# Attention stage: the last matmul of a dense bank and the bank's end are taken from the filler in one go

## The chip, the cores and the metric

One core of a Trainium2 chip runs the whole kernel. The metric is device time in microseconds (us), from one launch. The engines are PE (matmuls; its weight loads are shown apart, as PEld), DVE, ACT, POOL and SP; SP only issues transfers here.

## The reference

One encoder layer over 2048 tokens of width 1024, in float32. A vector `c` gives shift, scale and gate for two sub-layers. The first sub-layer projects the normalised input to queries, keys and values of 16 heads, 8 of them stick-breaking attention and 8 a chunked softmax attention over a band, and projects the joined outputs back; the second is a squared-ReLU MLP.

```python
h = rmsnorm(x, g_norm1) * (1.0 + sc1) + sh1
q_sb, k_sb, v_sb, q_ca, k_ca, v_ca = split(h @ w_in)
o_sb = stick_breaking_attention(q_sb, k_sb, v_sb)
o_ca = chunked_relpos_attention(rmsnorm(q_ca, g_q), rmsnorm(k_ca, g_k), v_ca, rel_bias)
x = x + gt1 * (concat(o_sb, o_ca) @ w_o)
h = rmsnorm(x, g_norm2) * (1.0 + sc2) + sh2
x = x + gt2 * (square(relu(h @ w1)) @ w2)
```

## The kernel before

The tokens are reversed and cut into four blocks of 512 (numbered g, or tb, 0 to 3). Each float32 operand is split into a high and a low part, and each product is three matmuls (high by high, high by low, low by high). The kernel runs in three stages.

In the **first** stage most of the projection is computed for blocks 3 and 2, and part of it for 1 and 0. In the **last** stage the output projection of block 0 runs, and then the MLP, in a form with fewer multiplications (seven products for eight).

Between them lies the **attention**. It is a list of 112 units (one head with one block of queries, and for stick-breaking also one block of keys), each of four steps, and a loop over 448 steps and 8 more that drain the pipeline. In each step PE gets, in this order: the transposes of weights from a unit some steps back (`transposes`, tile `wt`), the products with the values (`values`, tile `acc`), the scores of the next step (`scores`, tiles `z`, `ct`, `cz`), and then what `fill` puts there. DVE, ACT and POOL do the scan or the softmax and evict the transposes. The instructions of PE, ACT, DVE and POOL stay in the order of the program. The transfers issued in the attention by plain `nc.sync` have no such rule; those behind it (`osp`) have.

`fill` takes **dense** matmuls out of generators, the fillers: the projections that the first stage left (`fill_qkv`, twice: 288 matmuls for block 1 and 384 for block 0), and then the output projections of blocks 3, 2 and 1 (`outproj`, 192 matmuls each, eight rows of 24). A dense bank is one PSUM tile of 24 matmuls of 512 columns. The generator yields 1.0 behind each matmul; behind the 24th it yields a function, the bank's end, which evicts the bank. Two PSUM tiles serve as dense banks in turn. Some other yields are words: "wait" rests a step ahead of a new filler.

How many matmuls a step takes is counted in `credit`. Each step adds its share (`shares`, from a model of how much DVE and PE work the step has by itself), in proportion to the dense `work` that is still to be done; of older credit at most `CAP` = 5 is kept. `fill` then pulls from the generator while the credit is at least 1. When it pulls a bank's end, the function is put into `soon` (the jobs of the next step) and `rest = 1` stops the pulling for this step; the next `fill` lowers `rest` to 0 and goes on.

So there are two cases at the end of a bank. If credit is left after the 24th matmul, the bank's end is pulled in the same step. If less than 1 is left, the loop ends behind the 24th matmul; the next step's first pull then gets the bank's end, and that step rests and takes no dense matmul. Its share stays in the credit, up to the cap.

A bank's end of `fill_qkv` is `keep`: through `soon` and `heavy` an ACT copy of the bank is emitted, a step later the DVE subtraction and the store. That of `outproj` is `finish_row`: the DVE instruction `residual` on the row's tile, a store of the row, and for blocks 2 and 3 the sums of squares.

The total of dense matmuls that the attention is to take, `work`, is 14 x 48 + 480 = 1152, or 48 banks. That ends with row 3 of block 1's output projection. Rows 4 to 7 run behind the attention: `row()` pulls from the same generator until it gets one bank's end, and takes one matmul more. Between these calls stand the loads of the next stage's operands: `steps[0].fetch` (tiles `opm`), and the blocks of `right_blocks` (`some(k, n)`: n = 0 loads four tiles `ty`, for k = 0, or `cy`; n = 1 normalises them; n = 2 and 3 make the operands `h` of the MLP):

```python
steps[0].fetch(0, KT // 2)
row()
some(0, 0)
row()
steps[0].fetch(KT // 2, KT - 2)
some(0, 1)
row()
...
```

Of the kernel before, what the change touches and what calls it, by code (L numbers as in the profile page):

```python
# [24 lines left out]
KT = D // P  # L25
# [54 lines left out]
def encoder_kernel(ctx, tc, xs, c, g1, g2, w_in, w_first, w_rest, gqk, bias, w_o, w1, w2, w_ada, b_ada, out):  # L80
# [121 lines left out]
    def norm_apply(which, x, k, dst, pl, tg):  # L202

        j = 3 * which * KT + k
        a, b = aff[:, which, k : k + 1], mod[:, j : j + 1]
        hi, lo = dst[k][:, 0, :], dst[k][:, 1, :]
        act.activation(x, x, AF.Identity, scale=a, bias=b)
        act.copy(hi, x)
        return lambda: dve.tensor_tensor(lo, x, hi.bitcast(F32), op=ALU.subtract) and None
# [23 lines left out]
    def load_residual(g, n, pl):  # L233
        xr = temp(f"xr{g}_{n}") if drain else pl.tile([P, TB], F32, tag="xr", name=f"xr{g}_{n}")
        sp.dma_start(xr, xs[g, :, n])
        return xr
# [7 lines left out]
    if True:  # L244
# [371 lines left out]
        for k in range(KT):  # L616
# [5 lines left out]
            rest = norm_apply(0, xts[3][k], k, hts[3], np_, "a3") if k else None  # L622
            for j in ((KT + k + 1, k + 1) if k else (1,)) if k + 1 < KT else ():
                ada_column(j, adas[j])
                if rest:
                    rest = rest()
# [42 lines left out]
        credit = 0.0  # L669
# [67 lines left out]
    if True:  # L737
# [60 lines left out]
        def keep(u, o):  # L798

            os = fp.tile([P, 2, TB], F32R, tag="st", name=f"os{u.nm}")  # L800
            split(os[:, 0, :], os[:, 1, :], o, pool)
            q = pool if u.ca and u.g == 0 else sp
            q.dma_start(scr_m[u.g, u.ca * 4 + u.h // 2], os.bitcast(F32))
            if u.ca and u.h == NH - 1 and u.g > 0:
                filler.append(Filler(outproj, u.g))
# [240 lines left out]
        def fill_qkv(self, tb, ht, pieces):  # L1046
# [47 lines left out]
            for at, (n, j) in enumerate(banks):  # L1094
                piece, w = pieces[n], parts[n]
                last = at + 1 == len(banks) or not banks[at + 1][1]
                nm = f"f{tb}_{piece}_{j}"
                ps = dense.tile([P, TB], F32, tag="ps", name=f"p{nm}")
                cl = slice(j * P, (j + 1) * P)
                for k in range(KT):  # L1100
                    for m, job in plan.pop((at, k), ()):
                        parts[m].update(job())
                    if at + 1 == len(banks) and k in (0, 4):
                        yield "ahead"
                    for i, (a, b) in enumerate(((0, 0), (0, 1), (1, 0))):
                        flags = {"start": k == 0 and i == 0, "stop": k == KT - 1 and i == 2}
                        if piece in wide:
                            pe.matmul(ps, ht[k][:, b, cl], w[k][:, a, :], **flags)
                        else:
                            pe.matmul(ps, w[k][:, a, cl], ht[k][:, b, :], **flags)  # L1110
                        yield 1.0

                def keep(piece=piece, j=j, ps=ps, nm=nm, last=last):
                    if piece not in wide:
                        st = fp.tile([P, 2, TB], F32R, tag="st", name=f"st{nm}")
                        act.copy(st[:, 0, :], ps)
                        halves = [(st[:, 0, :], st[:, 1, :], ps)]
                    else:
                        if j % 2 == 0:
                            svs[:] = [  # L1120
                                fp.tile([P, NH // 2, 2, 2, HD], F32R, tag="st", name=f"sv{nm}_{hf}") for hf in range(2)
                            ]
                        halves = [
                            (
                                sv[:, :, j % 2, 0, :], sv[:, :, j % 2, 1, :],
                                ps[:, hf * CW : (hf + 1) * CW].rearrange("p (h d) -> p h d", d=HD),
                            )
                            for hf, sv in enumerate(svs)
                        ]
                        for hi, lo, half in halves:  # L1130
                            act.copy(hi, half)
                    parts = list(svs)

                    def rest():
                        for hi, lo, half in halves:
                            dve.tensor_tensor(lo, half, hi.bitcast(F32), op=ALU.subtract)
                        if piece not in wide:
                            at = (0, tb, piece % 2 * 2 + j)
                            to = scr_k[at].rearrange("l d t -> d l t") if piece // 2 else scr_q[at]
                            sp.dma_start(to, st.bitcast(F32))  # L1140
                        elif j % 2:
                            for hf, sv in enumerate(parts):
                                sp.dma_start(
                                    scr_v[piece // 6, tb, hf][:, :, j - 1 : j + 1, :].rearrange("h p t e -> p h (t e)"),
                                    sv.rearrange("p h t l d -> p h (t l d)").bitcast(F32),
                                )
                        if last:
                            have.add((piece, tb))

                    soon.append(rest)  # L1150

                keep.bank = True
                yield keep

        def outproj(self, g):
            def load(n):
                w = ring.tile([P, 2, KT, P], F32R, tag="r8", name=f"ow{g}_{n}")
                sp.dma_start(w.bitcast(F32), scr_wo[n,])
                return w

            self.loaders = [lambda n=n: load(n) for n in range(2)]
            yield lambda k: scr_m[g, k]
            mx = self.moving()
            ws = self.first()
            rx = load_residual(g, 0, xrp)
            yield "wait"
            for n in range(KT):
                w, xr = ws.pop(0), rx
                if g == 1:
                    resident[n] = w  # L1170
                if n + 2 < KT:
                    ws.append(load(n + 2))
                if n + 1 < KT:
                    rx = load_residual(g, n + 1, xrp)
                ps = dense.tile([P, TB], F32, tag="ps", name=f"po{g}_{n}")
                for k in range(KT):
                    if n + 1 == KT and k in (0, 4):
                        yield "ahead"
                    for i, (l, m) in enumerate(((0, 0), (0, 1), (1, 0))):
                        pe.matmul(  # L1180
                            ps, w[:, l, k, :], mx[k][:, m, :], start=k == 0 and i == 0, stop=k == KT - 1 and i == 2
                        )
                        yield 1.0
                yield lambda n=n, ps=ps, xr=xr: finish_row(g, n, ps, xr)

        def finish_row(g, n, ps, xr):
# [59 lines left out]
        def step_shares(units, work):  # L1246
# [32 lines left out]
            return [max(0.15, scale * v - t) for v, t in zip(vector, own)]  # L1279

        filler = [Filler(fill_qkv, 1, hts[1], (2, 3, 10, 0, 1)), Filler(fill_qkv, 0, None, (2, 3, 4, 10, 0, 1))]
        work = 14 * 48.0 + 5 * KT * KT * 3 / 2
        shares = step_shares(units, work)
        weight = sum(shares)
        credit = 0.0
        rest = 0
        late, soon, first, heavy, urgent = [], [], [], [], []

        def fill(part, more=0):

            nonlocal credit, rest, work, weight
            credit = min(credit, CAP) + part * (work - credit) / (weight * 0.95) + more
            weight -= part
            rest = max(0, rest - 1)
            while credit >= 1 and filler and not rest:
                got = next(filler[0].gen, None)
                if got is None:
                    filler.pop(0)
                elif got == "ahead":
                    for f in filler[1:2]:  # L1300
                        f.ahead()
                elif callable(got):
                    soon.append(got)
                    rest = 1
                elif got in RESTS:
                    rest = RESTS[got]
                else:
                    credit -= got
                    work -= got

        def force(f):

# [45 lines left out]
        for i in range(len(steps) + LAG):  # L1358
# [36 lines left out]
            if i + 1 < len(steps):  # L1395
                u, st = steps[i + 1]
                u.scores(st)
            fill(shares[i], turns.get(i, 0))
            later.tick()
        for u, j in late:  # L1400
# [26 lines left out]
    if True:  # L1427
# [610 lines left out]
        for mb in (1, 0):  # L2038
# [22 lines left out]
            if mb:  # L2061
# [11 lines left out]
                rest = len(steps)  # L2073
# [144 lines left out]
```

## Time and profile before

| | us |
|---|---|
| time, median of 3 runs (lowest, highest) | 2507.99 (2507.59, 2508.48) |
| profiled execution: its own time | 2507.11 |
| profiled execution: its span | 2505.4 |
| attention in the profile, first scores to last values | 410 to 1267 |

Of the span, PE is busy 2495.8 us, PEld 2095.3, DVE 2028.2, ACT 1527.0 and POOL 789.6. The granted clock is 0.999. The attention holds 672 dense matmuls into `pf` (the projections) and 480 into `po` (the output projections); 96 more into `po` follow it, between 1266.95 and 1288.8 us.

In the rows of the profile, nearly all instructions carry one line, that of a helper, so groups are told apart by their tiles. A PE row's duration is longer than the distance to the next start, because matmuls are pipelined: 512 columns are shown with some 390 ns, and the next matmul starts 227 ns later.

### The profile page before, as it was taken

To read this page: it belongs to the slowest core of one execution; us is meant where nothing else is said; L and a number is where in the kernel's file an instruction comes from. 1 tells how busy PE (TensorE), PEld (TensorE's weight loads), DVE (VectorE), ACT (ScalarE), POOL (GpSimd) and SP (SyncE) were. 2 spreads that over 40 slices of the span, in tenths; PEclk is the share of its full clock that TensorE was granted. 3 is DMA by queue.
4 is the path that set the end of the run, shared out by engine and by line. 5 is a ranking of instruction groups with operands and counts; after the bars stand their busy time and mean duration, and the time that the engine had idled before them with its cause. 6 is when DMAs were issued, how large, how long until landed. Compare 5 with 4: busy or idle time off the path is not lost.

```text
span 2505.4 us, 39519 instructions
## 1 busy us (share of the span) xinstructions
PE 2495.8 (100%) x12364; PEld 2095.3 (84%) x12364; DVE 2028.2 (81%) x3572; ACT 1527.0 (61%) x2928; POOL 789.6 (32%) x1175
## 2 busy tenths in 40 slices
PE   9999999999999999999999999999999999999999
PEld 8888888888888898888888888888888888888887
DVE  7656776897789888999877777779877859799998
ACT  6334434778876687666755555567555546577765
POOL 4330144777776677776720000000000000010100
PEclk9999999999999999999999999999999999999999
DMA  9879978789888788866787878996998996888982
GB/s 370 317 300 362 354 279 289 230 265 314 259 269 260 234 256 263 263 207 211 221 334 242 302 284 301 351 345 192 325 328 269 316 362 262 320 249 281 302 281 84
DMA packets 296114, 704.71 MB, mean 281 GB/s; under 512 B 32096, under 2 KB 88672, under 8 KB 284256
## 3 DMA queue, kind: packets, MB, share of 16 engines
q1 hardware_dynamic: 287552, 684.22, 79.2%
q0 software_dynamic: 6912, 13.63, 2.9%
q10 hardware_dynamic: 1440, 4.33, 0.4%
q8 instruction: 98, 1.61, 0.3%
q14 instruction: 112, 0.92, 0.1%
HBM read 473.99 MB, written 228.07 MB: 280 GB/s over the span
## 4 chain that ended last, share of the span: by engine, by line
PE 97%; DVE 2%; ACT 1%; issue 0%; DMA 0%; POOL 0%; SPq 0%; DVEq 0%; ACTq 0%; POOLq 0%
PE ps L42 29%; PE ps_s L42 17%; PE pt L42 11%; PE acc L42 8%; PE wt L42 7%; PE pf L42 6%; PE po L42 5%; PE z L42 5%; PE pq L42 3%; PE cz L42 2%; PE pso L42 2%; PE ct L42 1%; PE px L42 1%; DVE p L42 0%; DVE opr L42 0%
## 5 line engine op out<-in xcount | busy, mean ns | idle before, releaser
L42 ACT CAST wth<-wt 128x512 fp32r<-128x512 f32 (+3 forms) x544 | 257.8, 484 | 173.3 <-PE wt L42 160.9
L42 PE MATMUL ps<-h,opw 128*128 128x512 f32 x1512 | 358.6, 389 | 0.0
L42 POOL TENSOR_TENSOR b<-p 128x512 f32<-128x512 f32 (+1 forms) x320 | 292.6, 914 | 153.2 <-DVE p L42 97.2
L42 DVE TENSOR_TENSOR wtl<-wt,wth 128x512 fp32r<-128x512 f32 (+3 forms) x544 | 291.3, 547 | 60.5 <-ACT wth L42 56.1
L42 PEld LDWEIGHTS ps<-h,opw 128*128 128x128 f32 x1512 | 283.7, 188 | 58.8
L42 PE MATMUL pt<-w,ht 128*128 128x512 f32 x1248 | 288.1, 391 | 0.0
L42 PE MATMUL ps_s<-h,opw 128*128 128x512 f32 x1152 | 277.0, 389 | 0.0
L42 PEld LDWEIGHTS pt<-w,ht 128*128 128x128 f32 x1248 | 233.0, 188 | 47.5
L42 DVE TENSOR_TENSOR_SCAN p<-z,p,zero 128x512 f32<-128x512 f32 x192 | 245.2, 1278 | 18.6 <-ACT z L42 14.7
L42 PEld LDWEIGHTS ps_s<-h,opw 128*128 128x128 f32 x1152 | 216.0, 188 | 45.0
L42 ACT CAST opr<-r 128x512 fp32r<-128x512 f32 x280 | 174.3, 623 | 118.1 <-PE ps L42 65.6
L42 PE MATMUL acc<-wth,v 128*128 128x512 f32 (+3 forms) x544 | 221.2, 410 | 0.0
L42 PE MATMUL ps<-opr,ol 128*128 128x512 f32 x960 | 220.3, 389 | 0.0
L42 PEld LDWEIGHTS ps<-opr,ol 128*128 128x128 f32 x960 | 180.1, 188 | 37.8 <-DVE opr L42 0.4
L42 ACT ACTIVATE z<-z 128x512 f32<-128x512 f32 (+1 forms) x320 | 166.6, 521 | 52.7 <-PE z L42 48.9
L42 DVE TENSOR_TENSOR opr<-r,opr 128x512 fp32r<-128x512 f32 x280 | 185.7, 684 | 13.7 <-ACT opr L42 12.5
L42 PE MATMUL acc<-wtl,v 128*128 128x512 f32 (+3 forms) x544 | 185.5, 347 | 0.0
L42 PE MATMUL z<-k,q 128*128 128x512 f32 (+3 forms) x640 | 182.7, 367 | 0.6 <-DVE p L42 0.6
L42 POOL DMA_DIRECT2D scr_x<-txu x12 | 10.4, 869 | 543.5 <-ACT txu L42 541.6
L42 PE MATMUL ps<-oph,opv 128*128 128x512 f32 x768 | 174.9, 389 | 0.2 <-DVE txo L42 0.2
L42 PE MATMUL wt<-ident,b 128*128 128x128 f32 x1088 | 170.7, 272 | 0.4 <-DVE p L42 0.4
L42 PEld LDWEIGHTS ps<-oph,opv 128*128 128x128 f32 x768 | 144.1, 188 | 30.5 <-DVE txo L42 0.6
(238 smaller groups left out, 5064.6 us busy)
## 6 DMA issues: line engine op xcount, KB each, us to landing
r<-scr_hid SPq DMA_DIRECT2D x80, 512.0 KB, 7.5
q<-scr_q SPq DMA_DIRECT2D x128, 256.0 KB, 5.1
w<-in_w_dram SPq DMA_DIRECT2D x64, 512.0 KB, 5.7
k<-scr_k SPq DMA_DIRECT2D x240, 128.0 KB, 4.6
v<-scr_v SPq DMA_DIRECT2D x120, 256.0 KB, 4.3
wa<-in_w_ada_dram SPq DMA_DIRECT2D x48, 512.0 KB, 6.2
ow<-scr_wo SPq DMA_DIRECT2D x24, 1024.0 KB, 6.5
l<-scr_t SPq DMA_DIRECT2D x20, 1024.0 KB, 8.3
```

The source lines that it names most:

```text
L42: return lambda *x, **y: self.tc.keep_in_program_order(f(*x, **y))
```

## The change

The generators mark the last matmul of a bank, and `fill` pulls the bank's end together with it, whatever credit is left. The rest is then set in the step of the last matmul, and not in the step behind it. The matmul counts as one, as before.

```diff
@@ fill_qkv
-                        yield 1.0
+                        yield "last" if flags["stop"] else 1.0
@@ outproj
-                        yield 1.0
+                        yield "last" if k == KT - 1 and i == 2 else 1.0
@@ fill
                 elif got in RESTS:
                     rest = RESTS[got]
                 else:
-                    credit -= got
-                    work -= got
+                    credit -= 1
+                    work -= 1
+                    if got == "last":
+                        soon.append(next(filler[0].gen))
+                        rest = 1
```

`force`, which `row()` uses, is left as it was: it asks only whether what it got can be called.

## The prediction

> **What bounds the kernel now.** I read the page first, then the stages, then what PE waits for in the attention.
>
> ```profile
> span 2505.4 us, 39519 instructions
> PE 2495.8 (100%) x12364; PEld 2095.3 (84%) x12364; DVE 2028.2 (81%) x3572; ACT 1527.0 (61%) x2928; POOL 789.6 (32%) x1175
> ...
> PE 97%; DVE 2%; ACT 1%; issue 0%; DMA 0%; POOL 0%; SPq 0%; DVEq 0%; ACTq 0%; POOLq 0%
> ```
>
> PE is busy for all but 9.6 us of the span, and the chain that ended last is PE for 97%. The change adds and removes no matmul. So it can only win what PE loses by waiting, and can only cost what it makes PE wait. The next view gives the busy time of each engine (columns: PE, PEld, DVE, ACT, POOL, each with its instructions; then clock, share and rate of the DMAs) in the 856 us of attention and in 856 us of the last stage, which has nothing but dense matmuls on PE.
>
> ```profile
> 410.00:1266.00 856.00, 854.23 (x5005) 732.89 (x5004) 748.40 (x1511) 621.59 (x1338) 616.16 (x888) 1.00 0.80 250
> 1345.00:2201.00 856.00, 855.79 (x3789) 708.34 (x3788) 664.95 (x1082) 495.41 (x872) 21.07 (x30) 1.00 0.87 301
> ```
>
> In the attention PE is idle for 856.00 - 854.23 = 1.77 us. DVE is the next engine, with 748.40 / 856 = 87%. The view of PE's waits, for 405 to 1267 us, says who ends them (total, times, longest):
>
> ```profile
> PE z L42 <- DVE p L42: 0.6, 2, 0.3
> PE wt L42 <- DVE p L42: 0.4, 1, 0.4
> PE cz L42 <- DVE cols L42: 0.4, 1, 0.4
> ```
>
> DVE ends all that are listed; no transfer and no eviction of a dense bank is among them.
>
> **The change part by part.** First, how often it does anything. A step without dense matmuls, right behind a bank's 24th, is the case that it alters. Going through PE's timeline and counting `pf` and `po`, I find 19 such steps in the 456, at 48 bank ends. (Four more empty steps follow the end of a filler: there the rest is the new filler's own "wait", which stays. In other steps the share is below one matmul, which stays too.) The first of the 19 starts at 432.57, the last at 1205.21. PE's timeline (start, duration, instruction, count) at the first:
>
> ```profile
> 432.34 0.39 PE L42 MATMUL pf<-ht,fw 128*128 128x512 f32 x1
> 432.57 0.60 PE L42 MATMUL wt<-ident,b 128*128 128x128 f32 x4
> 432.93 0.48 PE L42 MATMUL acc<-wth,v 128*128 128x512 f32 x1
> 433.24 0.39 PE L42 MATMUL acc<-wtl,v 128*128 128x512 f32 x1
> 433.47 0.63 PE L42 MATMUL z<-k,q 128*128 128x512 f32 x2
> 433.94 0.49 PE L42 MATMUL wt<-ident,b 128*128 128x128 f32 x3
> ...
> 435.20 1.53 PE L42 MATMUL pf<-ht,fw 128*128 128x512 f32 x6
> 436.56 0.27 PE L42 MATMUL wt<-ident,b 128*128 128x128 f32 x1
> ```
>
> The reader is to see two things. The empty step takes 433.94 - 432.57 = 1.37 us, with no gap: each row begins where a row of its kind lets the next begin. And the step behind it takes six dense matmuls, twice the usual three: the share was carried, not lost. With the change these would be three and three. One dense matmul takes (436.56 - 435.20) / 6 = 0.227 us, so 3 x 0.227 = 0.68 us of PE work move one step ahead, and by that alone the time doesn't alter. At the last of the 19 it does:
>
> ```profile
> 1204.52 0.86 PE L42 MATMUL po<-fx,ow 128*128 128x512 f32 x3
> 1205.21 0.60 PE L42 MATMUL wt<-ident,e 128*128 128x128 f32 x4
> ...
> 1206.83 0.49 PE L42 MATMUL wt<-ident,e 128*128 128x128 f32 x3
> ...
> 1207.57 0.69 PE L42 MATMUL ct<-k,q 128*128 128x256 f32 x4
> 1208.62 0.62 PE L42 MATMUL cz<-k,q 128*128 128x384 f32 x2 [0.36 <-DVE cols L42]
> 1209.08 1.09 PE L42 MATMUL po<-fx,ow 128*128 128x512 f32 x4
> ...
> 1236.35 0.69 PE L42 MATMUL ct<-k,q 128*128 128x256 f32 x4
> 1236.88 0.51 PE L42 MATMUL cz<-k,q 128*128 128x384 f32 x2
> ```
>
> Without its dense matmuls PE runs ahead, and `cz` waits for a score bank that DVE has not read. From `ct` to `cz` it takes 1208.62 - 1207.57 = 1.05 us, against 1236.88 - 1236.35 = 0.53 us where nothing is late: 0.52 us lost, of which the profile calls 0.36 idle. Three matmuls more in the step at 1205.21 would bring PE there 0.68 us later, which covers the 0.52.
>
> **The gain** lies between nothing (all 19 like the first) and 19 x 0.52 = 9.9 us (all like the last). I take 1.2 us, two thirds of the 1.77 us that the profile calls idle in the whole stage, since that row is the nearest: some of the 1.77 stands at steps that the change doesn't touch.
>
> The other terms. A bank's end is emitted one step earlier in 19 cases: an ACT copy, a DVE subtraction and a store for a projection, one DVE instruction and a store for a row. No such instruction is added. They lie beside PE's matmuls, as the waits above show, and cost nothing; if that cover is gone, one of them delays a score bank by its own length, 0.75 us for a row's (1272.68 below). The loads of dense weights hang on positions within a bank and come at most a step earlier. I cost them at nothing; if a weight comes late, PE waits.
>
> The third term lies **at the end of the attention**. The 48th bank is row 3 of the last output projection. Its last matmul is taken in the last steps, its end before the change only by the first `row()`: DVE's timeline has `residual` of row 3 at once, of row 4 at 1272.68, of row 5 at 1278.84. After the change row 3's end is taken in the attention, so that each call of `row()` reaches one row further, and everything between the calls is queued a row later.
>
> ```profile
> 1272.68 0.75 DVE L42 SCALAR_TENSOR_TENSOR xr<-po,mod,xr 128x512 f32<-128x512 f32 x1 [5.31 <-PE po L42]
> 1276.41 2.51 DVE L42 TENSOR_TENSOR ty<-ty,r 128x512 f32<-128x512 f32 x4 [2.98 <-DMA ty<-scr_x]
> 1278.84 0.74 DVE L42 SCALAR_TENSOR_TENSOR txr<-po,mod,txr 128x512 f32<-128x512 f32 x1
> 1280.62 1.29 DVE L42 TENSOR_TENSOR h<-ty,h 128x512 fp32r<-128x512 f32 x2 [1.04 <-ACT h L42]
> ...
> 1289.45 2.63 DVE L42 TENSOR_TENSOR cy<-cy,r 128x512 f32<-128x512 f32 x4 [1.29 <-DMA cy<-scr_x]
> ...
> 1327.08 0.75 DVE L42 SCALAR_TENSOR_TENSOR cxr<-pso,mod,cxr 128x512 f32<-128x512 f32 x1 [1.89 <-PE pso L42]
> 1327.74 0.68 DVE L42 TENSOR_TENSOR opr<-w,opr 128x512 fp32r<-128x512 f32 x1
> ```
>
> ```profile
> 1259.07 1.80 SPq L42 DMA_DIRECT2D opm<-scr_m  x4
> ...
> 1267.03 1.98 SPq L42 DMA_DIRECT2D ty<-scr_x  x4
> 1272.67 0.32 SPq L42 DMA_DIRECT2D ow<-scr_wo  x1
> 1273.03 0.54 SPq L42 DMA_DIRECT2D txr<-in_xs_dram  x1
> ```
>
> ```profile
> 1266.95 22.00 PE L42 MATMUL po<-fx,ow 128*128 128x512 f32 x96
> 1288.80 16.48 PE L42 MATMUL pso<-opm,ow 128*128 128x512 f32 x72
> ...
> 1332.32 5.60 PE L42 MATMUL ps<-h,opr 128*128 128x512 f32 x24
> ```
>
> On SP the four `ty` loads pass behind the next row's `ow`, which waits for its buffer until 1272.67, and behind `txr`: they go out at about 1273.6 instead of 1267.03, 6.5 us later. From issue to DVE's first product took 1276.41 - 1267.03 = 9.4 us, so that product starts at about 1283. The last part of `h` for k = 0 is then queued behind row 7's `residual`, which waits for PE until 1288.80. I count k = 0 done near 1294.5, and the `cy` products of k = 1 there instead of at 1289.45: some 5 us late. k = 2 and 3 follow without a gap that could take this up, until the wait of 1.89 us at 1327.08. The first operand's DVE part, at 1327.74, would come some 3.2 us later and end at 1327.74 + 3.2 + 0.68 = 1331.6. PE needs it at 1332.32. So this costs nothing, by a margin of 0.7 us: if it is wrong by more, PE waits for the excess. What hides it is the 43.5 us of `pso` in front.
>
> **Sum**: 2507.11 (the profiled execution; 1.7 of it lies around the span) - 1.2 + 0 + 0 = 2505.9 us. The median of the runs stands 0.88 us above the profiled one, so the forecast for the median is 2507.99 - 1.2 = 2506.8 us.
>
> **The rivals.** *The empty steps are lost time.* If each had cost PE the 0.68 us of its share, the change would win 19 x 0.68 = 13 us: 2495. For it speaks only that the busy share can hide idling behind modelled ends. Against it are the burst of six, and start distances of 0.227 us in it. The Trainium skill (Perfetto Trace Analysis, Identifying the Most-Contended Engine) says that the matmul's busy share is a bad measure of how near PE is to its limit, and points to the weight loads' share instead. By that, 1 - 732.89 / 856 = 14% of the attention, over 100 us, could be free, and a large gain with it. The trace doesn't agree that this is headroom: the last stage, a plain stream of matmuls, shows 708.34 / 856 = 83%.
>
> *The late operand chain*, the one that ends slower. It decides from a lateness of 5 + 0.7, rounded up to 5.8 us, at k = 1. If the `ty` loads take their 9.4 us twice, because `opm` and `ow` are in flight as well, k = 0 ends 9.4 us later than I count, 5 + 9.4 - 5.8 = 8.6 us beyond the cover, and PE waits that long at 1332: 2506.8 + 8.6 = 2515.4. For it speaks that the queue is full there. Against it: four of the eight `opm` loads are out before 1267 already, since SP has nothing in front of them.
>
> *A late weight or a worse order elsewhere.* The attention's transfers are placed anew when matmuls move. One wait for a weight would be new; by the longest landing for `ty` above, under 9.4 us, in the middle 4: 2510.8. Against it: not one transfer is among PE's waits.
>
> *The change does nothing that counts.* DVE sets the pace at those waits, so what PE does not lose in the empty step it loses in the next: 2508.0. For it speaks DVE's 87%; against it, that nothing waits in the step behind 1209.08.
>
> **How the numbers follow.** Forecast (0 to 2.5 us gained): 0.68. Does nothing: 0.13. Late chain: 0.07. Late weight: 0.08. Lost time: 0.04. A measurement of this kernel can tell about 0.2%, 5.0 us, from no change. Faster than 2503.0: lost time, and a little of the forecast's upper bound of 9.9 us: 0.05. Slower than 2513.0: most of the late chain and the long end of the late weight: 0.07. The rest, 0.88, is within. The range reaches beyond the forecast into the 9.9 us, to 2503.5, and to the late weight's 2510.8, rounded to 2511.0; the late chain and the lost time lie outside.
>
> **What would show it.** Right: none of the 19 steps empty, no burst of six behind them, and some of the short waits such as that at 1208.62 gone; PE's idle time in the attention under 1.77 us; `ty` issued near 1273.6 and its product near 1283, and no wait of PE at the first `ps<-h,opr`. Wrong: an attention shorter by more than 2 us (hidden idling), PE idle before `ps<-h,opr` (late chain), or a transfer among PE's waits.

## The result and the profile after

The kernel became slower: 2513.51 us (median of 11 runs, 2512.78 to 2516.22) against 2507.99 us (11 runs). The ratio is 1.0024, 95% interval 1.0016 to 1.0032. The forecast was 2506.8 us, with a range from 2503.5 to 2511.0.

The page of the kernel after, to be laid beside that of before; the profiled execution took 2514.01 us:

```profile
span 2512.3 us, 39515 instructions
PE 2498.0 (99%) x12364; PEld 2096.3 (83%) x12364; DVE 2027.3 (81%) x3572; ACT 1527.8 (61%) x2928; POOL 788.6 (31%) x1175
...
PE 91%; DVE 4%; DMA 2%; ACT 2%; issue 1%; SPq 0%; POOL 0%; DVEq 0%; ACTq 0%; POOLq 0%
```

PE has the same 12364 matmuls. A part of the chain that ended last is now a transfer. The view of PE's waits, from the attention to 1290 us, names it:

```profile
PE po L42 <- DMA ow<-scr_wo: 4.2, 1, 4.2
PE z L42 <- DVE p L42: 0.6, 2, 0.3
PE wt L42 <- DVE p L42: 0.4, 1, 0.4
PE ct L42 <- DVE cols L42: 0.2, 1, 0.2
```

**The attention does what was forecast.** PE's timeline at the first and at the last of the 19 places:

```profile
432.08 0.40 PE L42 MATMUL pf<-ht,fw 128*128 128x512 f32 x1
432.32 0.60 PE L42 MATMUL wt<-ident,b 128*128 128x128 f32 x4
...
433.69 0.85 PE L42 MATMUL pf<-ht,fw 128*128 128x512 f32 x3
...
435.63 0.86 PE L42 MATMUL pf<-ht,fw 128*128 128x512 f32 x3
...
1205.68 0.86 PE L42 MATMUL po<-fx,ow 128*128 128x512 f32 x3
...
1207.11 0.69 PE L42 MATMUL ct<-k,q 128*128 128x256 f32 x4
1207.72 0.62 PE L42 MATMUL cz<-k,q 128*128 128x384 f32 x2
```

Three and three stand where none and six stood. From `ct` to `cz` it takes 0.61 us where it took 1.05. None of the 19 steps is empty. The four at the ends of fillers are, and so is one at 762.49, which takes no dense matmul in the kernel before either (762.65).

**The loss lies right behind it.** SP's timeline (start, duration, instruction, count), and PE's, at the end of the attention:

```profile
1266.49 0.32 SPq L231 DMA_DIRECT2D scr_x<-xr  x1
1266.86 1.87 SPq L42 DMA_DIRECT2D opm<-scr_m  x4
1268.83 0.52 SPq L42 DMA_DIRECT2D ow<-scr_wo  x1
1269.45 0.69 SPq L42 DMA_DIRECT2D txr<-in_xs_dram  x1
1271.77 0.32 SPq L42 DMA_DIRECT2D ow<-scr_wo  x1
1272.14 1.26 SPq L42 DMA_DIRECT2D txr<-in_xs_dram  x1
1273.46 4.51 SPq L42 DMA_DIRECT2D ty<-scr_x  x4
```

```profile
1266.06 11.12 PE L42 MATMUL po<-fx,ow 128*128 128x512 f32 x48
1281.35 12.72 PE L42 MATMUL po<-fx,ow 128*128 128x512 f32 x48 [4.18 <-DMA ow<-scr_wo]
1293.92 6.28 PE L42 MATMUL pso<-opm,ow 128*128 128x512 f32 x27
```

The four `opm` loads, out at 1259.07 before, now go out at 1266.86. In front of them stands `scr_x<-xr`, the store of row 3, which waits for DVE's `residual` of row 3:

```profile
1265.72 0.74 DVE L42 SCALAR_TENSOR_TENSOR xr<-po,mod,xr 128x512 f32<-128x512 f32 x1
```

That row ends at 1266.46, and the store goes out at 1266.49. Row 6's weights, `ow`, follow them at 1268.83, and PE has them 12.5 us later, at 1281.35. PE is done with row 5 at about 1277 and waits 4.18 us. Then it loses more: the 48 matmuls from 1281.35 take 1293.92 - 1281.35 = 12.57 us, where 48 x 0.227 = 10.9 us would do. The view of stretches shows why (length; PE, PEld, DVE, ACT and POOL busy, each with its instructions; then the granted clock as a share of full speed, the DMA share and the rate in GB/s):

```profile
1258.00:1267.00 9.00, 9.00 (x62) 8.12 (x61) 5.87 (x14) 7.70 (x19) 3.68 (x4) 1.00 0.34 117
1267.00:1275.00 8.00, 8.00 (x37) 6.59 (x36) 0.75 (x1) 1.13 (x2) 5.72 (x6) 1.00 0.95 323
1275.00:1290.00 15.00, 10.82 (x41) 8.52 (x40) 4.29 (x7) 3.62 (x6) 0.00 (x0) 0.89 1.03 417
1282.31:1285.72 3.41, 3.41 (x9) 2.64 (x8) 0.57 (x2) 0.00 (x0) 0.00 (x0) 0.50 1.02 393
```

The wait ends at 1281.35; from 1282.31 on the granted clock is 0.50 for 3.41 us. And the DMA engines stand two thirds idle between 1258 and 1267 us. The same view of the kernel before, in the first three stretches, for PE alone (length; PE busy; clock, DMA share, rate):

```profile
1258.00:1267.00 9.00, 9.00 (x65) 1.00 0.74 244
1267.00:1275.00 8.00, 8.00 (x38) 1.00 1.02 410
1275.00:1290.00 15.00, 15.00 (x68) 1.00 1.03 415
```

Share by length, the DMA engines work 0.74 x 9 + 1.02 x 8 + 1.03 x 15 = 30.3 us there before, and 0.34 x 9 + 0.95 x 8 + 1.03 x 15 = 26.1 us after: 4.2 us less, and PE waits 4.18. That the two figures agree so closely is no rule: in e2 below the same sum is 25.7 us, 4.7 less, and the wait is 3.6.

The account of the two profiled executions, span against span (+6.9 us): the start before the first scores -0.3, the attention -0.6, from there to the first `pso` +6.0 (by start distances 4.3 of wait and 1.7 of clock), the rest +1.8, nearly all of it two short waits in the last stage, at 1749.99 and 1960.40 (1.7 by start distances). The medians lie 5.5 us apart.

### The profile page after: what moved, and what is told of

Read it like the earlier page. It is cut to its first block, busy times and chain, and to the rows that moved or that the text cites. A ratio compares the mean times of both kernels' runs of the same rounds, so it can differ in the third digit from the quotient of the medians.

```text
span 2512.3 us, 39515 instructions
## 1 busy us (share of the span) xinstructions
PE 2498.0 (99%) x12364; PEld 2096.3 (83%) x12364; DVE 2027.3 (81%) x3572; ACT 1527.8 (61%) x2928; POOL 788.6 (31%) x1175
## 4 chain that ended last, share of the span: by engine, by line
PE 91%; DVE 4%; DMA 2%; ACT 2%; issue 1%; SPq 0%; POOL 0%; DVEq 0%; ACTq 0%; POOLq 0%
PE ps L42 25%; PE ps_s L42 16%; PE pt L42 11%; PE acc L42 8%; PE wt L42 7%; PE pf L42 6%; PE z L42 5%; PE po L42 5%; PE pq L42 3%; PE pso L42 2%; PE cz L42 2%; PE ct L42 1%; DMA hw<-in_w_dram 1%; PE px L42 1%; DMA ow<-scr_wo 0%
## 5 line engine op out<-in xcount | busy, mean ns | idle before, releaser
L42 DVE TENSOR_TENSOR opr<-r,opr 128x512 fp32r<-128x512 f32 x280 | 185.3, 682 | 13.8 <-ACT opr L42 12.5
L42 PEld LDWEIGHTS wt<-ident,b 128*128 128x128 f32 x1088 | 137.2, 140 | 39.3 <-DVE p L42 1.0
```

The costliest lines, as they stand in the source:

```text
L42: return lambda *x, **y: self.tc.keep_in_program_order(f(*x, **y))
```

## The experiments

Theory **S**: row 3's store, moved into the attention, stands in SP's queue ahead of the loads. Rivals: **D**, the denser attention makes transfers late; **R**, the shift of the rows against the loads fills the queue in front of `ow`; and, for the attention's share, **C** (shares are carried) against **L** (empty steps are lost).

| kernel | median us | before, run beside it | ratio, 95% interval | first scores to last values, us | wait for `ow`, us |
|---|---|---|---|---|---|
| e1 all but the last bank | 2506.85 | 2507.21 | 0.9998 (0.9989, 1.0006) | 856.06 | none |
| e2 the last bank only | 2513.40 | 2507.21 | 1.0025 (1.0016, 1.0035) | 856.64 | 3.6 |
| e3 store held back | 2506.68 | 2507.21 | 0.9998 (0.9990, 1.0007) | 855.93 | none |
| e4 fetch behind the row | 2513.07 | 2507.21 | 1.0022 (1.0013, 1.0032) | 856.04 | none |
| e5 store from ACT | 2507.36 | 2507.55 | 1.0001 (0.9992, 1.0010) | 856.09 | none |
| e6 rest one step longer | 2517.96 | 2507.55 | 1.0043 (1.0030, 1.0055) | 867.82 | none |
| e9 no rest | 2506.37 | 2507.46 | 0.9996 (0.9987, 1.0005) | 855.16 | none |
| e10 held back, late fetch | 2511.41 | 2507.46 | 1.0016 (1.0007, 1.0025) | 856.07 | none |
| e11 held back, half late | 2509.16 | 2507.46 | 1.0005 (0.9997, 1.0014) | 856.06 | none |
| e12 as e3 | 2507.29 | 2507.46 | 0.9999 (0.9990, 1.0008) | 855.92 | none |

The lengths of the attention go from start to start. In that column the kernel before has 856.61 us, and 856.53 in its second profile (e7); the kernel after has 855.97, and 855.98 in its second (e8).

### Which bank: e1 and e2

```diff
-                    if got == "last":
+                    if got == "last" and work > 0:      # e1
+                    if got == "last" and work == 0:     # e2, else as before
```

> The change for 47 banks; the 48th bank's end (row 3 of the last output projection) is left to the first row(), as before. Theory S (the loss is row 3's store, which stands in SP's queue ahead of the four opm loads and so ahead of row 6's weights): PE does not wait for ow, opm goes out before 1260 us, and the 0.9 us won by the attention stay: 2507.1 us. Theory D (the denser attention itself makes transfers late): PE still waits some 4 us for ow, 2513 us. If the two waits of 0.6 and 0.8 us at the first matmuls of the last stage (near 1749 and 1959 us after the change) come from the end of the attention, they are gone too; if from the denser attention, they stay: 2508.5 us.

> The kernel before, with the 48th bank's end alone taken together with its last matmul. S: the whole loss, without the gain of the attention: PE waits some 4 us for ow, then runs some 4 us at about half its clock, 2508.0 + 6.0 = 2514 us. D: no wait, 2508.0 us.

e1 keeps the shorter attention (by 0.5 us, for 0.9 expected) and loses nothing behind it; e2 is the whole loss without the gain. D falls: the one bank of 48 that stands at the end of the attention makes the loss. e2 waits 3.6 us, until 1280.69, and has half the clock for 6.8 us, from 1279.37 on. The short waits of e1 in the last stage were not settled by this; see e7 and e8.

### The store or the shift: e3

```diff
         def finish_row(g, n, ps, xr):
             residual(g, n, ps, xr)
-            if g < 2 and drain:
+            if g < 2 and (drain or (g, n) == (1, 3)):
                 return
```

> After the change, but row 3's store is kept in the list of stores, as those of rows 4 to 7 are, and goes out behind row 5. The rows stay shifted by one against what stands between the calls of row(). S: opm goes out before 1260, ow of row 6 at about 1265.3, PE does not wait for it, 2507 us, if the late operand chain of the prediction is covered. R (the shift of the rows fills the queue in front of ow): PE waits as after the change, 2513 us.

The rows stay shifted, the store goes out at 1274.88, and the loss is gone. SP's timeline of e3:

```profile
1257.56 1.47 SPq L42 DMA_DIRECT2D opm<-scr_m  x3
1264.23 0.32 SPq L42 DMA_DIRECT2D ow<-scr_wo  x1
1264.65 0.38 SPq L42 DMA_DIRECT2D txr<-in_xs_dram  x1
1270.74 0.32 SPq L42 DMA_DIRECT2D ow<-scr_wo  x1
1271.11 1.41 SPq L42 DMA_DIRECT2D txr<-in_xs_dram  x1
1272.57 2.21 SPq L42 DMA_DIRECT2D ty<-scr_x  x4
```

`opm` is out before 1260 (the stretch shown holds three of the four loads), and row 6's `ow` at 1264.23. R falls. PE doesn't wait at the first `ps<-h,opr` either: the later operand chain of the prediction is covered, as it said. The first operand's DVE part ends there at 1329.26 and PE starts at 1330.39.

### Order or amount: e4 and e5, e10 and e11

e4 leaves the store where it is and moves the loads:

```diff
-        steps[0].fetch(0, KT // 2)
         row()
+        steps[0].fetch(0, KT // 2)
```

> After the change, with the first four opm loads moved behind the first row(). The store of row 3 still stands first in SP's queue, but ow of row 6 is next. S, in its reading that the 2 MB of opm in front of ow make it late, and not the store's wait of some 0.8 us: no wait for ow, 2507 to 2508 us; opm is out by 1275, early enough for 1288. If the store's own wait is what counts: still a wait for ow of some 3 us, 2512 us.

A miss. The wait for `ow` is gone, but the time lost is still there. PE's waits in e4 behind the attention, those for loads:

```profile
PE pso L42 <- DMA wo<-scr_wo: 1.8, 1, 1.8
PE pso L42 <- DMA opm<-scr_m: 1.5, 3, 0.9
```

The loss moved to later loads. So it isn't only that 2 MB stand in front of `ow`. That suggests that 2 MB come late into a stretch that has no DMA time to spare, and gave theory **Q**: what is lost is the idle time of the DMA engines ahead of 1267 us, and the store matters only because it makes them idle.

e5 issues the store at the same place from ACT's queue (`act.dma_start(scr_x[g, n], xr)` for row 3):

> After the change, with row 3's store issued at the same place by ACT instead of SP. S (what costs is that the store waits for DVE at the head of SP's queue): opm goes out before 1260 us, the DMA share between 1258 and 1267 us is above 0.7 again (0.34 after the change), PE does not wait for ow: 2506.7 us. If the store itself, as a transfer ahead of ow, is what costs: PE still waits, 2513 us.

SP's timeline of e5, and its stretch ahead of 1267 us:

```profile
1258.39 1.85 SPq L42 DMA_DIRECT2D opm<-scr_m  x4
1265.54 0.32 SPq L42 DMA_DIRECT2D ow<-scr_wo  x1
```

```profile
1258.00:1267.00 9.00, 9.00 (x64) 8.18 (x63) 6.15 (x15) 7.13 (x17) 3.70 (x5) 1.00 0.88 291
```

The transfer is the same; only SP doesn't wait at it. The share is 0.88 and the loss is gone. The Trainium skill (DMA: Bandwidth & Descriptors, Issuing engines are not separate DMA queues) says that issuing from several engines gives no bandwidth, since all share the same 16. That agrees: from 1267 to 1275 and to 1290 us the engines move 410 and 415 GB/s before, and 388 and 375 in e5. What e5 wins is not bandwidth but that nothing is held up behind a store that isn't ready.

e10 and e11 put Q to the test without any store in front: e3, with four or two of the `opm` loads behind the first `row()`.

> e3 with the first four opm loads behind the first row(): no store stands in front of them, they are only issued later. Theory Q (what costs is the time that the DMA engines stand idle between 1258 and 1267 us in front of a stretch in which they have no time to spare; the store is only what makes them idle): the DMA share there falls to some 0.3 as after the change, and PE waits 4 to 5 us behind 1267, at whichever load comes last: 2512 us. Theory S in its narrow form (the store ahead of the loads): no wait, 2507 us.

> As e10, with two of the four opm loads (1 MB) behind the first row() and two in front. Q: half of the 2 MB is late, some 2.5 us of DMA time at 400 GB/s, so between nothing (what slack there is covers it) and 2.5 us lost: 2507 to 2510 us, and less than e10. If the order of the loads counts and not their sum: as e10.

Against e12 (2507.29 us), 1 MB late (e11) costs 1.9 us and 2 MB late (e10) cost 4.1 us. The first two stretches of e12, e11 and e10, in this order, with the columns as above:

```profile
1258.00:1267.00 9.00, 9.00 (x63) 8.16 (x62) 6.10 (x15) 7.58 (x18) 3.70 (x5) 1.00 0.84 286
1267.00:1275.00 8.00, 8.00 (x37) 6.59 (x36) 0.75 (x1) 1.34 (x3) 5.96 (x6) 1.00 0.98 375
1258.00:1267.00 9.00, 9.00 (x64) 8.13 (x62) 6.01 (x15) 7.67 (x18) 3.70 (x5) 1.00 0.80 243
1267.00:1275.00 8.00, 8.00 (x37) 6.62 (x36) 0.75 (x1) 1.26 (x3) 5.86 (x6) 1.00 0.82 298
1258.00:1267.00 9.00, 9.00 (x63) 8.08 (x62) 5.82 (x14) 7.70 (x19) 3.69 (x4) 1.00 0.42 136
1267.00:1275.00 8.00, 8.00 (x37) 6.62 (x36) 0.75 (x1) 1.08 (x2) 5.68 (x6) 1.00 0.80 295
```

With the shares of 1.00, 1.00 and 1.01 from 1275 to 1290 us, the engines work 30.4 us there in e12, 28.8 in e11 and 25.3 in e10: 1.6 us less for 1.9 lost, and 5.1 less for 4.1 lost. The waits of e10 stand at `opm` (1.2 us), at `wo` (0.3) and at the operand chain (1.3), that of e11 only there:

```profile
1344.48 3.03 PE L42 MATMUL ps_s<-h,opw 128*128 128x512 f32 x12 [1.48 <-ACT cp L42]
```

S in its narrow form falls with e10: the loads need no store in front of them to cost time. Q holds in both in direction and in time. It was wrong on the place: in e11 the idle DMA time lies between 1267 and 1275 us, and not ahead of 1267. It gives no exact price either, and whether another order of the loads would spare e11 its late operand chain was not tried.

> e3 unchanged, beside the others: 2506.7 us; 0.6 us shorter attention than before, no wait for ow, and so 0.3 to 1.3 us under the kernel before.

e12 gives e3's time again within 0.6 us, so that differences of that size between these medians say nothing.

### What an empty step costs: e6 and e9

e6 lets the rest last one step more at all 47 ends (`rest = 2`), the 48th as in e1:

> The change for 47 banks, end of the attention as before, and the rest behind each bank's end lasts one step more, so that some 47 steps take no dense matmul where there were 19 before the change and none of that kind after it. Theory C (shares are carried, an empty step costs only the waits that it lays bare): the change won 0.9 us over 19 steps, 0.05 us for each, so 47 cost some 2.2 us against e1: 2509 us. Theory L (each empty step loses its share of 0.68 us): 47 x 0.68 = 32 us, 2539 us. If DVE sets the pace there and nothing depends on it: 2506.9 us.

C and L both missed: 867.82 - 856.06 = 11.8 us, neither 2.2 nor 32. In e6's PE timeline I added up what the start distances exceed the median ones of the same kind by (from 0.05 us on) in the empty step and the one behind it: behind a step with one dense matmul 0.33 us each on the mean (16 places), with two 0.16 (18), with three 0.11 (11), with four none (2); 9.3 us together. The worst place lies outside this count, where two empty steps stand in a row and PE runs ahead of DVE:

```profile
871.02 0.40 PE L42 MATMUL pf<-fx,fw 128*128 128x512 f32 x1
...
876.50 0.61 PE L42 MATMUL cz<-k,q 128*128 128x384 f32 x2 [1.73 <-DVE wtl L42]
876.95 2.01 PE L42 MATMUL po<-fx,ow 128*128 128x512 f32 x8
```

Here the rest of e6 and the new filler's own add up. By the same count the empty places of the kernel before cost about as much each (0.28 us behind one matmul, 0.11 behind three, none behind four). C was wrong in taking its price from what the change had won: of the waits at an empty step, most came back in the steps behind it (see the gain, below). Why nothing of the kind is won back in e6 stays open.

e9 is e3 without any rest at a bank's end (`rest = int(work == 0)`):

> e3 without the rest at a bank's end: the step of the last matmul goes on into the next bank with what credit it has left. In e3 the waits over 0.1 us in the two steps behind a bank's end, added up, are 1.1 us. Theory C (thin steps lay waits bare): up to 1.1 us less than e3 in the attention, 2506 us. If nothing but the empty steps mattered: as e3.

The attention is 0.8 us shorter than in e3, within the 1.1 that C allowed, and 1.4 us shorter than before. e9 has the lowest median of all, 2506.37 us, but its interval holds 1: it can't be told from the kernel before by its time, only by its attention.

### The short waits of the last stage: e7 and e8

> The kernel before, unchanged, for a second profile. Two short waits of PE in the last stage, at 1749 and 1959 us, are in the profile after the change, one of them in e1 and e3 too, none in the profile before and in e2. If the denser attention makes them, this profile has none; if they come and go by themselves, it may have one.

> The kernel after, unchanged, for a second profile: the wait for ow is there again, 3.5 to 4.5 us, and half the clock for 3.4 or 6.8 us behind it; of the two short waits near 1749 and 1959 us at least one, if the denser attention makes them.

The kernel before had a wait of 0.5 us there in its second profile (`ps_s` for DVE's `cp`), none in its first; the kernel after 1.1 us in its first and 0.4 in its second. The one near 1959 is in the kernel before (e7) and in seven other profiles, but not in the first of the kernel before, nor in e2, e5, e6 and e10: it comes and goes. The one near 1749 is in both profiles of the kernel after and in e10, and in no other. What makes either was not found. The wait for `ow` came again in e8, 3.8 us, with half the clock for 6.8 us, from 0.8 us ahead of its end on.

## Why the prediction was wrong

**What bounds the kernel.** Right: PE bounds it, and the change could only move waits. The loss is one wait and the half clock that follows it.

**How often the change acts, and what an empty step is.** Right: 19 places, three and three for none and six, the four rests of new fillers left. The share is carried. Only that 1.05 us falls to 0.61, and not to 0.53, was a shade less than I said.

**The gain of the attention.** Right in its mechanism, half in size: 1.2 us forecast, 0.6 us measured (from 856.5 to 856.6 in three profiles without the change of the 47 banks, to 855.9 to 856.1 in nine with it alone; PE's idle time in the stage from 1.77 to 1.49 us). The mis-sized term is the share of the waits that the change really removes. At 18 of the 19 places (the other, near 762, keeps an empty step), by the count of e6, the empty step and the one behind it lose 2.5 us before and 0.7 after, but the three steps behind these lose 1.0 before and 2.1 after; e7 and e8 give 2.6, 0.7, 1.0 and 2.2. So 1.8 us of waits went and 1.1 came back within three steps: what PE does not lose in the empty step it loses, for the larger part, a little later.

**Evictions and weights in the attention.** Right: no transfer and no eviction of a dense bank is among PE's waits in the attention after.

**The end of the attention: the step that failed.** The prediction saw that row 3's end moves into the attention, followed the DVE chain and the `ty` loads, and put "So this costs nothing". It let one instruction out that the moved function issues: row 3's own store. It had named "a store for a row" among the bank's ends that come earlier, put them all at nothing, and did not ask what stands behind that store in SP's queue. Before, `drain` was set when the row ended, so the store was kept in the list and went out at 1276.38 us; in the attention it goes out at once, in front of the `opm` loads, where it waits for DVE. The sentence "four of the eight `opm` loads are out before 1267 already, since SP has nothing in front of them" was true of the kernel before only. e3 and e5 show it: with the store held back, or issued from ACT, PE does not wait there. In the place of nothing stand 4.2 us of wait and some 1.7 us of half clock.

**The rivals.** Late weight: the right place for the loss, but "by the longest landing for `ty`" priced at 4 us; the wait was that long, and what came on top, the clock, no step of the prediction had. Late operand chain: covered in e3, where the `ty` loads went out at 1272.57 and their first product came at 1280.61. In the kernel after they went out at 1273.46 for 1273.6 forecast, and the product came at 1285.65 for 1283, since they too landed late; PE was late itself by then and did not wait. It is the wait in e11, though at a later operand (`opw`, 1344.48) than the one that the prediction named. At the one it named, PE starts in e11 at 1331.96, the DVE part ends at 1332.11, and PE doesn't wait: the cover was larger than the 0.7 us counted. Lost time: excluded, the attention is 0.6 us shorter and not 13. Does nothing: excluded by the length of the attention, though not by any median; its mechanism, that PE loses the time a little later, holds for some 1.1 of 1.8 us.

**The chances.** Slower by over 0.2% had 0.07. The late cases were given little because no transfer was among PE's waits; but the DMA share of 1.03 behind 1267 us was in the profile, and was a sign that a load that came late there would have little to make it up with.

## What to carry to other kernels

When a piece of code moves across the end of a stage, list everything it issues, stores first: a store that isn't ready holds up every load behind it in its queue. Where the DMA engines are full from some point on, idle DMA time ahead of it was not made up here (e4, e10), and moving the loads about moved the wait; issue as much as there is room for in the quiet stretch before. A planner's empty step did not cost its share here, only waits that it laid bare, so look at which engine is next before paying to fill it.

## What the hardware showed unexpectedly

A wait can cost more than its length. Half the clock was granted for 3.41 or 6.83 us around or behind the end of the waits of 4.2 (after), 3.6 (e2) and 3.8 us (e8), and also behind one of 1.80 us in e4 (0.66 on the mean between 1321 and 1326 us); not behind 1.73 us in e6 or 1.48 us in e11. In the kernel after that is 1.7 us on top of 4.2.

The clock changes in a run lie whole multiples of 3.41 us apart, and in that grid the traces from the attention on sort by PE's idle time in one stretch of 3.41 us. With 1.80 (e4), 2.32 (e2), 2.46 (after) and 2.95 us (e8) the next stretch had half the clock. With 1.72 (after, the stretch before), 1.48 (e11) and 1.30 us (e6, whose 1.73 us lie across two stretches) it had the full one. Full clock came back behind the first stretch without a wait; in e2 and e8 a first half-clock stretch still held 1.32 and 0.82 us of wait, and a second one followed. So in these runs the limit lay between 0.50 and 0.53 of a stretch. The Trainium skill (TensorE: Matmul & The Clock Gate, What's actually happening) states that the clock falls after at least one idle window of some 3.4 us. The stretches of 3.41 us agree with such a window; the 1.80 us do not agree with one that must be idle throughout.
